# A hybrid mixer layer: one buffer for xdt and for B's two parts, and buffers of their own for B's returning tile and the transposed blocks

## The chip, the cores and the metric

The kernel runs on one core of a Trainium2 chip. The metric is the device time of one execution in microseconds, as the median of three runs. A profile is one further execution, taken by the hardware profiler.

## What is computed

One layer of a streaming encoder for two groups of requests that share the weights: 256 new positions of one stream and 16 positions of each of 8 running streams, 384 rows in all, with 2048 channels.

```python
u = rmsnorm(x);  proj = u @ w_in          # pool | z | xBC | dt | gates
a_pool = pooling of windows 2, 4, 8, 16, a map per group, a scale per channel
xbc = silu(causal_conv(xBC) + b)          # 4 taps; x: 4096 channels, B and C: 8 groups of 128
# for each chunk, group g, head r (8 groups, 8 heads of 64 channels each):
xdt = x * dt
y = einsum(cb * decay, xdt) + einsum(C, h) * exp(cum)
h = h * exp(last) + einsum(B, w_end, xdt)
y = y + d_skip * x
a_ssd = rmsnorm over each group of 512 (y * silu(z)) * ssd_norm
m = sig(gA) * (a_pool @ w_pool_proj) + sig(gB) * (a_ssd @ w_ssd_proj)
x = x + rmsnorm(m @ w_out);  x = x + rmsnorm(relu(rmsnorm(x) @ w_up)**2 @ w_down)
```

Outputs are the new x of both groups of requests and the new states of pooling, convolution and scan.

## The kernel before

All products are in float32, made of three matmuls of two parts each: every weight tile of 128x1024 is fetched by SP's queue (`wfetch`, line 63), its high part is written by ScalarE (`wh`, line 70), its low part by VectorE (`wl`, line 71), and `mm3` (lines 98 to 100) multiplies high by high, high by low and low by high. The tiles w, wh and wl have three buffers each. One projection (`proj`) takes two such weights, 24 matmuls each.

The profile's stage from about 430 us to 1210 us is a loop over the 8 groups of the scan (line 860). A group projects six convolution tiles (x 0, x 1, B, C, x 2, x 3) and four z tiles. TensorE's order is written out by hand: a chain (`last`, `lump`, `behind`) puts each block of small matmuls behind the projection before it. Each group has two such blocks:

- the middle block, after the projection of x 2: `t_pp` of the previous group's pair 1, `t_cb` (B times C), `t_yT` and `t_Y` of that pair, `t_yi` of this group's pair 0, and the state products `su` (`state`, line 794);
- the end block, after z 3: `t_pp`, `t_yT`, `t_Y` of pair 0, `t_yi` of pair 1, `su` of pair 0.

`finish(prev)` (line 842) stands after z tile 1. It normalises the previous group: TensorE sums over the partitions (`bc_g`, lines 196 and 197), VectorE reads that sum (`ssum<-bc_g`, line 199), takes ten Newton instructions (lines 182 to 186) and scales the four tiles `zs` (line 847).

Blocks of x and of B have to be transposed so that positions lie on partitions. `turned` does it in steps that `tick` runs, one after each weight of a projection: VectorE transposes blocks of 32x32 (`xb`, line 612), POOL's queue writes them to DRAM in four DMAs (line 617), and POOL's queue reads the whole tile back (line 623) into `xT` for x, and for B into the low half of `Bhl`. From `xT`, `xside` (line 742) makes `xdt` and `xhl` on VectorE, and sends a part of `xhl` through DRAM to `xst` on SP's queue. `bside` (line 706) splits B into `Bhl`'s two parts (ScalarE line 708, VectorE line 709) and sends a part through DRAM to `bst` in the same way. `mside` (line 729) reads the PSUM bank of `t_cb` into `cbm`. `eside` makes the decay matrices `E`, `dside` scales the old state `hs`.

All tiles of this stage come from the pool `pd`, which gives two buffers to a tag unless another number is named: two for `xdt`, two for `Bhl`, and two for `cacc`, which the convolution's taps (lines 593 to 598) and the transposed blocks `xb` share.

What is not in TensorE's chain is ordered by the framework's scheduler when the program is built: it orders each engine's queue by its own estimate of when inputs and buffers are ready. `later()` keeps an instruction behind the last split weight. On the chip every engine then takes its queue in this order.

Of the kernel before, what the change touches and what calls it, by code (L numbers as in the profile page):

```python
# [6 lines left out]
F32 = mybir.dt.float32  # L7
F32R = mybir.dt.float32r
I32 = mybir.dt.int32
AF = mybir.ActivationFunctionType  # L10
ALU = mybir.AluOpType
# [3 lines left out]
P = 128  # L15
T = 384
# [17 lines left out]
def build(ctx, tc, io):  # L34
    nc = tc.nc
    v, s, te, gp, sy = nc.vector, nc.scalar, nc.tensor, nc.gpsimd, nc.sync
# [13 lines left out]
    def mmtile(name):  # L50
        return psm.tile([P, 512], F32, tag="mm", name=name)
# [163 lines left out]
    def in_units(i):  # L215
        return [win[i - 5, 0], win[i - 5, 1]]
# [145 lines left out]
    with tc.tile_pool(name="phc", bufs=1, reuse_waits="tile") as pc, tc.tile_pool(name="phc2", bufs=2, reuse_waits="tile") as pc2:  # L362
        pst = pc.tile([P, KD, NB, 15], F32, name="pst")
        gp.dma_start(pst, io["state_pool"])
        bufs = []
        for i in range(2):
            b = pc.tile([P, 640], F32, name=f"pbuf{i}")[:, :519]
# [190 lines left out]
    with tc.tile_pool(name="phd", bufs=2, reuse_waits="tile") as pd, tc.tile_pool(  # L558
        name="phd1", bufs=1, reuse_waits="tile"
# [4 lines left out]
        for i in range(3):  # L564
            b = pd1.tile([P, 24, 19], F32, name=f"cbuf{i}")
# [38 lines left out]
        def conv(ui, c, tag, nb):  # L604
            return taps(conv_in(ui, c), c, tag, nb)

        def turned(src, i, o):
            xb, scr = [], t_scr[i]

            def turn():  # L610
                xb.append(pd.tile([P, T], F32, tag="cacc", name=f"xb{i}"))
                v.transpose(xb[0], src)

            def spread():
                for q in range(4):
                    p32 = slice(q * 32, q * 32 + 32)
                    gp.dma_start(
                        scr[:, p32].rearrange("(j a) b -> a j b", a=32),
                        xb[0][p32].rearrange("p (j b) -> p j b", b=32),
                    )  # L620

            wait = [lambda: None] if i < 32 else []
            steps.append(wait + [turn, spread, lambda: gp.dma_start(o, scr.rearrange("(b t) n -> t b n", b=3))])

        def xturned(D, g, j):
            S = D.p[j // 2]
            if j % 2 == 0:
                S.xT = pd.tile([P, 2, 3, P], F32, tag="xT", name=f"xT{S.nm}", bufs=1)
            turned(D.xs[j], g * 4 + j, S.xT[:, j % 2])
# [74 lines left out]
            return i  # L704

        def bside(D):
            bh, bl = (D.Bhl[:, a].rearrange("p b n -> p (b n)") for a in range(2))
            s.activation(bh, bl.bitcast(F32), AF.Copy)
            v.tensor_tensor(bl, bl.bitcast(F32), bh.bitcast(F32), ALU.subtract)
            bscr = b_scr[D.g]  # L710
            sy.dma_start(bscr, D.Bhl[:, :, 2, :].bitcast(F32))
            D.bs = bst[D.g % 2]
            for p4 in range(4):
                for h2 in range(2):
                    sy.dma_start(
                        D.bs[h2 * 64 + p4 * 16 : h2 * 64 + p4 * 16 + 16].bitcast(F32),
                        bscr.rearrange("(q h r) l n -> h l r q n", q=4, h=2)[h2, p4 // 2],
                    )
# [21 lines left out]
            )  # L740

        def xside(S):
            S.xdt = pd.tile([P, 2, 3, P], F32, tag="xdt", name=f"xdt{S.nm}")
            for q in range(2):
                tv = S.xT[:, q].rearrange("p b (h q) -> p b h q", h=2)
                for o, i in ((S.xdt, 3), (S.xT, 6)):
                    v.tensor_tensor(
                        o[:, q].rearrange("p b (h q) -> p b h q", h=2),
                        tv,
                        tok[:, i : i + 3, S.h0 + q * 2 : S.h0 + q * 2 + 2].unsqueeze(3).to_broadcast([P, 3, 2, 64]),  # L750
                        ALU.mult,
                    )
            S.xhl = pd.tile([P, 2, 2, 3, P], F32R, tag="xhl", name=f"xhl{S.nm}", bufs=1)
            s.activation(S.xhl[:, 0], S.xT, AF.Copy)
            v.tensor_tensor(S.xhl[:, 1], S.xT, S.xhl[:, 0].bitcast(F32), ALU.subtract)
            xscr = x_scr[S.qd]
            for l in range(2):
                sy.dma_start(xscr[:, l], S.xhl[:, l, :, 2, :].bitcast(F32))
            S.xst = pd.tile([P, 4, 2 * P], F32R, tag="xst", name=f"xst{S.nm}", bufs=1)
            for p4 in range(4):  # L760
                for h2 in range(2):
                    sy.dma_start(
                        S.xst[h2 * 64 + p4 * 16 : h2 * 64 + p4 * 16 + 16].bitcast(F32),
                        xscr.rearrange("(q h r) l j n -> h l r q (j n)", q=4, h=2)[h2, p4 % 2],
                    )
# [20 lines left out]
        def dside(S):  # L786
            v.tensor_tensor(
                S.hs.rearrange("p b (h q) -> p b h q", h=4),
                S.hs.rearrange("p b (h q) -> p b h q", h=4),
                decb[:, S.h0 : S.h0 + 4, :].rearrange("p h b -> p b h").unsqueeze(3).to_broadcast([P, NB, 4, 64]),  # L790
                ALU.mult,
            )
# [75 lines left out]
        for g in range(G + 1):  # L868
            if g == G:
                xside(prev.p[1])  # L870
                eside(prev.p[1], 0)
                eside(prev.p[1], 1)
                dside(prev.p[1])
                gate_b(0, pd, "hs")
                py = mmtile("pp_last")
                lump(lambda: t_pp(prev.p[1], py))
                lump(lambda: t_yT(prev.p[1]))
                lump(lambda: t_Y(prev.p[1]))
                state(prev.p[1])
                final(prev.p[1])  # L880
                gate_b(1, pd, "hs")
                finish(prev)
                break
            u0 = 17 + g * 10
            D = Pair()
            D.g = g
            D.p = [pair(D, jp) for jp in range(2)]
            D.xs, D.zs = [], []
            D.Bhl = pd.tile([P, 2, 3, P], F32R, tag="Bhl", name=f"Bhl{g}")
            D.xs.append(conv(u0, g * 4, "xs", 6))  # L890
            if g:
                xside(prev.p[1])
            xturned(D, g, 0)
            pload(D.p[0])
            if g:
                eside(prev.p[1], 0)
            D.xs.append(conv(u0 + 1, g * 4 + 1, "xs", 6))
            xturned(D, g, 1)
            if g:
                eside(prev.p[1], 1)  # L900
            D.BT = conv(u0 + 2, 32 + g, "BT", 2)
            turned(D.BT, 32 + g, D.Bhl[:, 1].bitcast(F32))
            if g:
                dside(prev.p[1])
            cload(D.p[0])
            D.CT = conv(u0 + 3, 40 + g, "CT", 2)
            cside(D)
            b2 = conv_in(u0 + 4, g * 4 + 2)
            S = D.p[0]
            S.py = mmtile(f"py{S.nm}")  # L910
            if g:
                lump(lambda: t_pp(prev.p[1], S.py))
            lump(lambda: t_cb(D))
            bside(D)
            if g:
                lump(lambda: t_yT(prev.p[1]))
                lump(lambda: t_Y(prev.p[1]))
            lump(lambda: t_yi(S))
            mside(D)
            yside(S)  # L920
            if g:
                state(prev.p[1])
                final(prev.p[1])
            D.xs.append(taps(b2, g * 4 + 2, "xs", 6))
            xside(S)
            xturned(D, g, 2)
            D.xs.append(conv(u0 + 5, g * 4 + 3, "xs", 6))
            xturned(D, g, 3)
            eside(S, 0)

            def zproj(j):
                ps = proj(in_units(u0 + 6 + j), xg, f"z{g}_{j}")
                z = pd.tile([P, T], F32, tag="zs", name=f"zs{g}_{j}", bufs=7)
                with later():
                    v.tensor_tensor(halves(z), even_odd(ps), halves(rstd), ALU.mult)
                    s.activation(z, z, AF.Silu)
                D.zs.append(z)

            zproj(0)
            pload(D.p[1])  # L940
            eside(S, 1)
            zproj(1)
            if g:
                finish(prev)
            zproj(2)
            dside(S)
            cload(D.p[1])
            zproj(3)
            S1 = D.p[1]
            S1.py = mmtile(f"py{S1.nm}")  # L950
            lump(lambda: t_pp(S, S1.py))
            lump(lambda: t_yT(S))
            lump(lambda: t_Y(S))
            lump(lambda: t_yi(S1))
            yside(S1)
            state(S)
            final(S)
            prev = D
# [92 lines left out]
    with tc.tile_pool(name="phf", bufs=1, side="right", reuse_waits="tile") as pf, tc.tile_pool(  # L1051
        name="phf2", bufs=2, side="right", reuse_waits="tile"
# [240 lines left out]
    with tc.tile_pool(name="phg", bufs=1, reuse_waits="tile") as pg, tc.tile_pool(  # L1293
        name="phg2", bufs=2, reuse_waits="tile"
# [8 lines left out]
        for c8 in range(NC):  # L1303
            hh = []
            for f8 in range(8):
                f = c8 * 8 + f8
# [172 lines left out]
```

## Time and profile before

| | |
|---|---|
| runs | 2692.59 us median of 3 (2689.98 to 2694.77) |
| profiled execution | 2697.46 us; span from its first to its last instruction 2695.3 us |
| mean granted clock of TensorE | 0.992 of full speed |
| TensorE busy | 2650.0 us, 98% of the span |
| VectorE, ScalarE, GpSimd busy | 1523.1, 1186.8, 269.6 us |

A line of the order of time gives the start in us from the span's start, how long the instruction (or the run of equal ones) lasted, the engine, the line of the kernel, the operation with output and inputs, and in brackets how long the engine had been idle before it and what ended that. A line of the waits gives the engine, what it was about to do, whom it waited for, the total in us, how often, and the longest. A line of a group gives count, busy time, mean ns, and the idle time before. A line of DMA issues ends with KB and the median us to landing.

### The profile page before, as it was taken

Reading aid. Unit: us, or ns where it says so; the run is one execution under the profiler, and the core shown is the slowest. Engines: PE = TensorE matmul, PEld = TensorE weight load, DVE = VectorE, ACT = ScalarE, POOL = GpSimd, SP = SyncE. Lnnn points to the kernel's source line nnn. Section 1 sums busy time; section 2 is a strip of 40 time slices with the busy share of each in tenths; the row PEclk is TensorE's granted clock in tenths of the full one; section 3 lists DMA queues with packets and bytes.
Section 4 is the critical chain, followed back from the end, with each engine's and each line's share of the span. In section 5 each row is a group of like instructions: output and inputs, shape, how many; then the busy total and the mean of one; then the engine's idle time right before and its main releaser. Section 6 shows DMA issues by size and latency. Waiting matters only on the chain.

```text
span 2695.3 us, 38595 instructions
## 1 busy us (share of the span) xinstructions
PE 2650.0 (98%) x15149; PEld 2468.2 (92%) x15149; DVE 1523.1 (57%) x2148; ACT 1186.8 (44%) x1834; POOL 269.6 (10%) x366
## 2 busy tenths in 40 slices
PE   9999999999999999999999999999999999999998
PEld 8998889999989999988888888989999999999897
DVE  6585336687887888866433345634444444444446
ACT  6443235466566665644322234633233333333233
POOL 0000001233233233321000000000000000000000
PEclk9999999999999999999999999999999999999999
DMA  7444446676766676666644455344444444444443
GB/s 270 152 133 158 145 150 212 202 224 214 237 216 227 222 249 211 224 211 227 217 156 157 156 187 155 126 135 139 133 136 138 133 136 138 133 134 139 134 134 132
DMA packets 153846, 467.10 MB, mean 173 GB/s; under 512 B 21121, under 2 KB 48321, under 8 KB 148673
## 3 DMA queue, kind: packets, MB, share of 16 engines
q1 hardware_dynamic: 134400, 389.90, 44.6%
q0 software_dynamic: 19264, 74.74, 7.9%
q8 instruction: 119, 1.95, 0.3%
q14 instruction: 63, 0.51, 0.1%
HBM read 414.97 MB, written 49.58 MB: 172 GB/s over the span
## 4 chain that ended last, share of the span: by engine, by line
PE 56%; DMA 1%; DVE 1%; POOL 0%; issue 0%; ACT 0%; DVEq 0%; POOLq 0%; ACTq 0%
PE pj_up L98 6%; PE pj_up L100 6%; PE pj_up L99 6%; PE wd L150 6%; PE wd L151 6%; PE wd L149 6%; PE pj_sp L151 3%; PE pj_sp L150 3%; PE pj_sp L149 3%; PE pj_gb L149 2%; PE wo L149 2%; PE wo L151 2%; PE pj_gb L150 2%; PE pj_gb L151 2%; PE wo L150 2%; DMA t_scr<-xb 1%
## 5 line engine op out<-in xcount | busy, mean ns | idle before, releaser
L98 PE MATMUL pj_up<-x1h,wh_up 128*128 128x384 f32 (+1 forms) x1024 | 334.1, 326 | 0.0
L99 PE MATMUL pj_up<-x1l,wh_up 128*128 128x384 f32 (+1 forms) x1024 | 333.9, 326 | 0.0
L100 PE MATMUL pj_up<-x1h,wl_up 128*128 128x384 f32 (+1 forms) x1024 | 333.8, 326 | 0.0
L71 DVE TENSOR_TENSOR wl_wd<-w_wd,wh_wd 128x1024 fp32r<-128x1024 f32 x126 | 154.4, 1225 | 240.3 <-ACT wh_wd L70 240.3
L151 PE MATMUL wd<-wh_wd,hl 128*128 128x512 f32 x756 | 286.8, 379 | 0.0
L150 PE MATMUL wd<-wl_wd,hh 128*128 128x512 f32 x756 | 286.8, 379 | 0.0
L149 PE MATMUL wd<-wh_wd,hh 128*128 128x512 f32 x756 | 286.8, 379 | 0.0
L70 ACT ACTIVATE wh_wd<-w_wd 128x1024 fp32r<-128x1024 f32 x126 | 133.1, 1056 | 322.2 <-PE wd L151 261.7
L70 ACT ACTIVATE wh_up<-w_up 128x1024 fp32r<-128x1024 f32 x126 | 133.1, 1057 | 291.8 <-PE pj_up L99 231.8
L98 PE MATMUL pj_x<-xgh,wh_x 128*128 128x384 f32 x768 | 256.2, 334 | 0.0
L71 DVE TENSOR_TENSOR wl_up<-w_up,wh_up 128x1024 fp32r<-128x1024 f32 x126 | 154.4, 1225 | 177.8 <-ACT wh_up L70 177.7
L100 PE MATMUL pj_x<-xgh,wl_x 128*128 128x384 f32 x768 | 254.0, 331 | 0.1
L99 PE MATMUL pj_x<-xgl,wh_x 128*128 128x384 f32 x768 | 254.0, 331 | 0.0
L99 PEld LDWEIGHTS pj_up<-x1l,wh_up 128*128 128x128 f32 x1024 | 194.0, 189 | 0.2
L98 PEld LDWEIGHTS pj_up<-x1h,wh_up 128*128 128x128 f32 x1024 | 194.0, 189 | 0.2
L100 PEld LDWEIGHTS pj_up<-x1h,wl_up 128*128 128x128 f32 x1024 | 194.0, 189 | 0.0
L100 PE MATMUL pj_z<-xgh,wl_z 128*128 128x384 f32 x512 | 170.9, 334 | 16.1 <-DVE wl_z L71 16.1
L98 PE MATMUL pj_z<-xgh,wh_z 128*128 128x384 f32 x512 | 169.7, 331 | 0.0
L99 PE MATMUL pj_z<-xgl,wh_z 128*128 128x384 f32 x512 | 169.6, 331 | 0.0
L71 DVE TENSOR_TENSOR wl_sp<-w_sp,wh_sp 128x1024 fp32r<-128x1024 f32 x64 | 78.4, 1225 | 154.0 <-ACT wh_sp L70 154.0
L151 PEld LDWEIGHTS wd<-wh_wd,hl 128*128 128x128 f32 x756 | 143.2, 189 | 20.0
L150 PEld LDWEIGHTS wd<-wl_wd,hh 128*128 128x128 f32 x756 | 143.2, 189 | 19.8
(335 smaller groups left out, 6044.9 us busy)
## 6 DMA issues: line engine op xcount, KB each, us to landing
w_up<-w_up SPq DMA_DIRECT2D x128, 512.0 KB, 3.3
w_wd<-w_down SPq DMA_DIRECT2D x128, 512.0 KB, 3.3
w_x<-w_in SPq DMA_DIRECT2D x96, 512.0 KB, 4.2
w_z<-w_in SPq DMA_DIRECT2D x64, 512.0 KB, 4.4
w_sp<-w_ssd SPq DMA_DIRECT2D x64, 512.0 KB, 3.3
w_ga<-w_ga SPq DMA_DIRECT2D x32, 512.0 KB, 3.4
w_pp<-w_pp SPq DMA_DIRECT2D x32, 512.0 KB, 3.3
hs<-ssm POOLq DMA_DIRECT2D x16, 1024.0 KB, 6.8
```

Source lines behind the costliest of these rows:

```text
L70: cut[0] = s.activation(h, w, AF.Copy)
L71: cut[1] = v.tensor_tensor(l, w, h.bitcast(F32), ALU.subtract)
L98: te.matmul(out, wh, xh, start=first, stop=False, **how)
L99: te.matmul(out, wh, xl, start=False, stop=False, **how)
L100: return te.matmul(out, wl, xh, start=False, stop=last, **how)
L149: te.matmul(out, mh, vh, start=k == 0, stop=False)
L150: te.matmul(out, mh, vl, start=False, stop=False)
L151: last[0] = te.matmul(out, ml, vh, start=False, stop=k == nk - 1)
```

## The change

The tag of the transposed blocks becomes `xb`, so that they have two buffers of their own and `cacc` serves the taps alone. `xdt` and `Bhl` have one buffer each. B's returning tile is no longer read into the low half of `Bhl`, but into a tile `Bt` of its own; `Bhl` is allocated only in `bside`, which writes both parts from `Bt`. The call of `bside` moves from the middle block, behind `t_cb`, to behind the convolution of x 3. Matmuls, DMAs and instructions are the same in number and size.

```diff
             def turn():
-                xb.append(pd.tile([P, T], F32, tag="cacc", name=f"xb{i}"))
+                xb.append(pd.tile([P, T], F32, tag="xb", name=f"xb{i}"))
                 v.transpose(xb[0], src)
...
         def bside(D):
-            bh, bl = (D.Bhl[:, a].rearrange("p b n -> p (b n)") for a in range(2))
-            s.activation(bh, bl.bitcast(F32), AF.Copy)
-            v.tensor_tensor(bl, bl.bitcast(F32), bh.bitcast(F32), ALU.subtract)
+            D.Bhl = pd.tile([P, 2, 3, P], F32R, tag="Bhl", name=f"Bhl{D.g}", bufs=1)
+            s.activation(D.Bhl[:, 0], D.Bt, AF.Copy)
+            v.tensor_tensor(D.Bhl[:, 1], D.Bt, D.Bhl[:, 0].bitcast(F32), ALU.subtract)
...
         def xside(S):
-            S.xdt = pd.tile([P, 2, 3, P], F32, tag="xdt", name=f"xdt{S.nm}")
+            S.xdt = pd.tile([P, 2, 3, P], F32, tag="xdt", name=f"xdt{S.nm}", bufs=1)
...
             D.xs, D.zs = [], []
-            D.Bhl = pd.tile([P, 2, 3, P], F32R, tag="Bhl", name=f"Bhl{g}")
             D.xs.append(conv(u0, g * 4, "xs", 6))
...
             D.BT = conv(u0 + 2, 32 + g, "BT", 2)
-            turned(D.BT, 32 + g, D.Bhl[:, 1].bitcast(F32))
+            D.Bt = pd.tile([P, 3, P], F32, tag="Bt", name=f"Bt{g}", bufs=1)
+            turned(D.BT, 32 + g, D.Bt)
...
             lump(lambda: t_cb(D))
-            bside(D)
...
             D.xs.append(conv(u0 + 5, g * 4 + 3, "xs", 6))
+            bside(D)
             xturned(D, g, 3)
```

## The prediction

> **What bounds the kernel now.** I read the page's engine row first, then who waited for whom on TensorE, then the order of time around each of those waits.
>
> ```profile
> PE 2650.0 (98%) x15149; PEld 2468.2 (92%) x15149; DVE 1523.1 (57%) x2148; ACT 1186.8 (44%) x1834; POOL 269.6 (10%) x366
> ...
> PE pj_z L100 <- DVE wl_z L71: 16.1, 7, 5.1
> PE su L802 <- DVE cbm L731: 14.9, 6, 4.7
> PE cb L652 <- ACT xs L601: 2.7, 2, 2.5
> ```
>
> TensorE sets the time. It waits in the group loop only, for three things: a low half of a z weight (7 waits, 16.1 us), the PSUM bank that `mside` reads (6 waits, 14.9 us) and a convolved tile (2.7 us). A change to buffers can save these waits and what hangs on them, and no more; it can also make new ones.
>
> How much hangs on them shows in the starts of the block's first product, `t_pp` (two blocks in a group, one after the x projections of four tiles, one at the group's end).
>
> ```profile
> 510.75 0.83 PE L696 MATMUL py<-xhl,Bhl 128*128 128x256 f32 x6
> 554.25 0.83 PE L696 MATMUL py<-xhl,Bhl 128*128 128x256 f32 x6
> ...
> 559.52 0.43 PE L98 MATMUL pj_x<-xgh,wh_x 128*128 128x384 f32 x1
> ...
> 583.19 0.33 PE L197 MATMUL bc_g<-nl_g,onesr 128*128 128x384 f32 x1
> 585.30 0.43 PE L100 MATMUL pj_z<-xgh,wl_z 128*128 128x384 f32 x1 [1.46 <-DVE wl_z L71]
> ...
> 600.68 0.83 PE L696 MATMUL py<-xhl,Bhl 128*128 128x256 f32 x6
> ...
> 681.02 0.33 PE L197 MATMUL bc_g<-nl_g,onesr 128*128 128x384 f32 x1
> 681.64 0.43 PE L100 MATMUL pj_z<-xgh,wl_z 128*128 128x384 f32 x1
> ...
> 1075.15 0.83 PE L696 MATMUL py<-xhl,Bhl 128*128 128x256 f32 x6
> 1118.65 0.83 PE L696 MATMUL py<-xhl,Bhl 128*128 128x256 f32 x6
> 1172.05 0.83 PE L696 MATMUL py<-xhl,Bhl 128*128 128x256 f32 x6
> ```
>
> From the end block to the middle block it is 43.50 us early and late in the loop (510.75 to 554.25, 1075.15 to 1118.65): nothing is lost there. From the middle block to the end block it is 46.43 us in group 1, of which the z wait takes 2.11 where an undisturbed group takes 0.62 (681.02 to 681.64); so 44.9 is the clean length. Groups 1 to 7 together take 1172.05 - 510.75 - 7 x 43.50 = 356.8 us for this stretch, against 7 x 44.9 = 314.6 clean. **42.2 us** are lost in these seven groups, more than the waits themselves.
>
> **Where the old waits come from.**
>
> ```profile
> 747.17 0.56 DVE L709 TENSOR_TENSOR Bhl<-Bhl 128x384 fp32r<-128x384 f32 x1 [4.44 <-ACT Bhl L708]
> ...
> 749.31 0.69 DVE L731 TENSOR_TENSOR cbm<-cb,cst 128x512 f32<-128x512 f32 x1
> ...
> 750.05 0.80 PE L802 MATMUL su<-xst,bst 64*128 64x256 f32 x3 [4.30 <-DVE cbm L731]
> ...
> 775.91 0.56 DVE L747 TENSOR_TENSOR xdt<-xT,tok 128x384 f32<-128x384 f32 x1 [4.07 <-DMA xT<-t_scr]
> 776.98 2.35 DVE L71 TENSOR_TENSOR wl_z<-w_z,wh_z 128x1024 fp32r<-128x1024 f32 x2
> ...
> 483.60 0.56 DVE L747 TENSOR_TENSOR xdt<-xT,tok 128x384 f32<-128x384 f32 x1 [4.54 <-DMA xT<-t_scr]
> ...
> 485.94 0.69 PE L100 MATMUL pj_z<-xgh,wl_z 128*128 128x384 f32 x1 [5.09 <-DVE wl_z L71]
> ...
> 489.30 0.33 PE L98 MATMUL pj_z<-xgh,wh_z 128*128 128x384 f32 x1
> ```
>
> VectorE takes its queue in order. At 747 it stands 4.44 us at `bside`'s split, whose input is still on its way through DRAM, and `cbm`, queued behind, comes out late; `su` needs the bank that `cbm` reads. At 776 and 484 it stands 4.07 and 4.54 us at `xside`'s product, whose transposed tile has not landed, with the low halves of the z weights behind it.
>
> **What the change removes.** On VectorE's queue in the changed program, `Bhl`'s split no longer stands ahead of `cbm`; it comes after the third tap of tile 2. The single `xdt` buffer keeps pair 1's product from being placed before the end block's `t_Y` has read pair 0's, so it stands behind the second read of Y in that block, when its tile has long landed. The `xb` tag lets a transposition go ahead without a free `cacc`. So VectorE stands at none of the three places any more. I take the whole 42.2 us of groups 1 to 7 away, and in group 0 the z wait of 5.09 us with its aftermath: 485.94 to 489.30 is 3.36 us for ten matmuls, which start 0.16 to 0.17 us apart elsewhere (1242.40 and 1242.57 below), 1.7 us too long, so 6.8 us. The wait for the convolved tile in group 0 stays: the order ahead of it is as before. Removed: 42.2 + 6.8 = **49.0 us**.
>
> **What the change adds.** The same scheduling that keeps `xdt` and `Bhl` back has moved something else. In the program before, VectorE's queue holds, after `nl_g` and pair 1's first product, the low halves of z tile 2's two weights, then zs 1, then the read of the norm's broadcast sum (`ssum<-bc_g`), with the Newton steps spread among later weights. In the changed program, in all seven groups with a `finish`, the queue reads: E, zs 0, `nl_g`, a transposition, `ssum<-bc_g`, the ten Newton instructions in one piece, two of the four scalings `zs<-zs,vec,ny_g`, and only then z tile 2's first low half. TensorE's queue is unchanged there: `bc_g` runs after z tile 1's last matmul and z tile 2's first follows it at once. TensorE therefore reaches its third z matmul 0.62 us after `bc_g`, and the weight for it is split behind a chain that starts from `bc_g`. Nothing can hide that chain; it is a new wait in each of seven groups, with a fixed length, whichever engine was early.
>
> Its length, from the same chain at the loop's end:
>
> ```profile
> 1242.40 0.33 PE L196 MATMUL bc_g<-nh_g,onesr 128*128 128x384 f32 x1
> 1242.57 0.33 PE L197 MATMUL bc_g<-nl_g,onesr 128*128 128x384 f32 x1
> ...
> 1242.93 0.56 DVE L199 TENSOR_SCALAR ssum<-bc_g 128x384 f32<-128x384 f32 x1 [1.89 <-PE bc_g L197]
> 1243.52 0.36 DVE L182 TENSOR_SCALAR ny_g<-ssum 128x384 int32<-128x384 int32 x1
> 1243.92 0.56 DVE L184 TENSOR_TENSOR na_g<-ny_g 128x384 f32<-128x384 f32 x1
> ...
> 1249.50 0.55 DVE L184 TENSOR_TENSOR na_g<-ny_g 128x384 f32<-128x384 f32 x1
> 1250.09 0.56 DVE L185 TENSOR_TENSOR na_g<-na_g,ssum 128x384 f32<-128x384 f32 x1
> ...
> 1251.28 2.21 DVE L847 SCALAR_TENSOR_TENSOR zs<-zs,vec,ny_g 128x384 f32<-128x384 f32 x4
> ...
> 1040.55 1.22 DVE L71 TENSOR_TENSOR wl_z<-w_z,wh_z 128x1024 fp32r<-128x1024 f32 x1
> ```
>
> `bc_g` to `ssum` 0.36; `ssum` to the first Newton instruction 0.59; that one to the next 0.40; nine dependent steps at 0.59 (1249.50, 1250.09, 1251.28) 5.31; two scalings at (2.21 - 0.61) / 3 = 0.53 each, 1.06; the split 1.22; TensorE's start behind it some 0.05. Sum 8.99 us, where 0.62 is the normal distance: **8.4 us** lost per group.
>
> A wait of that size has an aftermath. The rows at 485.94 and 489.30 gave 1.7 us; the 4.75 us wait of group 2 is followed by this:
>
> ```profile
> 654.88 0.69 PE L98 MATMUL pj_x<-xgh,wh_x 128*128 128x384 f32 x1
> ...
> 660.06 0.33 PE L99 MATMUL pj_x<-xgl,wh_x 128*128 128x384 f32 x1
> ```
>
> Sixteen matmuls in 5.18 us instead of 2.6: 2.6 us lost. I take the middle, 2.1 us. So each group pays 8.4 + 2.1 = 10.5, seven groups **73.5 us**. [...]
>
> **What is moved and costs nothing.** VectorE between `cbm` and z tile 0's second low half:
>
> ```profile
> 1029.45 0.69 DVE L731 TENSOR_TENSOR cbm<-cb,cst 128x512 f32<-128x512 f32 x1
> ...
> L787 DVE TENSOR_TENSOR hs<-hs,decb 128x2048 f32<-128x2048 f32 x16 | 36.6, 2289 | 0.0
> ...
> 758.82 6.12 SPq L762 DMA_DIRECT2D xst<-x_scr  x6
> w_z<-w_in SPq DMA_DIRECT2D x64, 512.0 KB, 4.4
> ```
>
> From 1029.45 to the end of the split at 1040.55 + 1.22 it is 12.3 us. The new queue takes the 2.29 us state scaling out of it and puts five 0.56 us instructions (two `xdt`, two `xT`, `Bhl`) and a transposition in: about 12.9. `cbm` can start about 2.3 us after the middle block's first product (its input 1.7 us, one split ahead), so the half is ready at 15.2; TensorE wants it at 5.27 (554.25 to 559.52) plus three halves of 24 matmuls at 0.16, 17.3. Two us to spare; if that cover were gone, each us over would cost one per group. On SP's queue, z tile 2's loads now stand behind `b_scr`, `x_scr`, eight `xst` and eight `bst` transfers. These can start once `xhl` is split, about 14 us after that product; with 4.4 us for a landing, 16 issues at up to 1.02 (6.12 / 6) and another 4.4 for the weight, it is there at 39 at the worst. The chain reaches its split at 28.9 + 7.7 = 36.7, so the cover holds unless the issues go at their slowest; at half of 1.02 the weight is there at 31. POOL's queue only takes the state load and some spreads in another order. The end block's VectorE gains three 0.56 us products and loses a 0.95 us split ahead of the next weight; the 43.50 us stretch has no wait today and I keep it.
>
> **The sum.** 73.5 - 49.0 = +24.5 us. The profiled execution took 2697.46 us (span 2695.3), 4.9 above the median of the runs, 2692.59; its waits for DMA may have been longer than theirs. Added to the profiled one it is 2722, to the median 2717. Since the new wait is fixed while the old ones vary, I take the place between: **2719 us**.
>
> **Rivals.** First, faster: the waits for DMA go and the Newton chain is covered, as would be if z tile 2's split stood ready before `bc_g`; then the whole 49 us are gained, 2644. It decides from the point where that split precedes `ssum` on VectorE's queue. Against it stands the queue's order in all seven groups; only if TensorE had other work between `bc_g` and z tile 2, 8 us of it, could the price vanish, and its queue has none. 0.05, and 0.03 that partial relief just balances it. Second, slower still: part of the old waits remains, with VectorE late at z tile 0 or `Bt` not landed when ScalarE's copy comes up, some 2 us a group with 0 to 1 of aftermath: 7 x 2 to 3 = 14 to 21, 2733 to 2740. For it speaks the cover of only 2 us; against it that the new wait lets VectorE's and SP's backlog drain in every group. 0.12. Third, SP: z tile 2's weight lands after the chain, by the 2 us at the worst above and a split: 7 x 3 = 21, 2740. 0.04. My forecast keeps 0.76.
>
> **Range and chances.** The low end is the median's sum with the short aftermath, 2717 - 3, less 8 for a chain that runs tighter and for the spread of the runs (2689.98 to 2694.77): 2706. The high end takes in the long aftermath and part of the second rival: 2738. A measurement of this kernel can tell about 0.2%, 5 us. Slower takes the forecast and the last two rivals, 0.92.
>
> **What would show it.** In the profile after: TensorE's waits for `cbm` gone; VectorE's waits for `xT` gone in groups 1 to 7; TensorE waiting seven times about 8 us at line 100 of `pj_z` for `wl_z`, some 58 us in all, each followed by matmuls of 0.53 us; the stretch from middle to end block near 55.4 us, the other still 43.5. I am wrong if that wait is below 5 us, or if waits at other lines add up to over 10 us.

## The result, and the profile after

The changed kernel takes **2719.35 us** (median of 4 runs, 2718.74 to 2722.5) against 2692.88 before (4 runs, 2689.98 to 2694.77): a ratio of 1.0102, 95% interval 1.0084 to 1.0119. The forecast was 2719. The profiled execution took 2718.74 us with a span of 2717.0, 21.7 more than the span before, where the forecast had 24.5.

The page's engine row and TensorE's waits in the group loop, changed kernel:

```profile
PE 2650.7 (98%) x15149; PEld 2466.1 (91%) x15149; DVE 1525.3 (56%) x2148; ACT 1166.5 (43%) x1820; POOL 272.3 (10%) x366
...
PE pj_z L100 <- DVE wl_z L71: 27.9, 8, 4.6
PE pj_z L98 <- ACT wh_z L70: 27.7, 8, 4.7
```

TensorE's busy time and its instructions are those of before (2650.0 us). The waits of `su` for `cbm` and of `cb` are gone. In their place stands a double wait in z tile 2: at line 98 for the high half of its first weight, at line 100 for the low half. The forecast had a single one, at line 100.

The order of time on TensorE, first products of the blocks, and `t_pp` of the loop's end:

```profile
501.68 0.83 PE L696 MATMUL py<-xhl,Bhl 128*128 128x256 f32 x6
545.18 0.83 PE L696 MATMUL py<-xhl,Bhl 128*128 128x256 f32 x6
600.24 0.83 PE L696 MATMUL py<-xhl,Bhl 128*128 128x256 f32 x6
...
1138.15 0.83 PE L696 MATMUL py<-xhl,Bhl 128*128 128x256 f32 x6
1193.59 0.83 PE L696 MATMUL py<-xhl,Bhl 128*128 128x256 f32 x6
1229.37 0.83 PE L696 MATMUL pp_last<-xhl,Bhl 128*128 128x256 f32 x6
```

From end block to middle block it is 43.50 us as before. From middle to end block it is 55.06 us in group 1 and 55.44 in group 7; the five between lie at 55.18 to 55.50. Together the seven take 1193.59 - 501.68 - 7 x 43.50 = 387.4 us, 30.6 more than before. Group 0 starts the count 510.75 - 501.68 = 9.07 us earlier, and the stretch behind the loop is 0.1 longer. 30.6 - 9.07 + 0.1 = 21.6, the whole difference of the spans.

One of these groups in the order of time, several engines:

```profile
742.42 0.83 PE L696 MATMUL py<-xhl,Bhl 128*128 128x256 f32 x6
...
760.50 5.12 SPq L762 DMA_DIRECT2D xst<-x_scr  x8
766.14 3.59 SPq L715 DMA_DIRECT2D bst<-b_scr  x7
769.84 1.36 SPq L63 DMA_DIRECT2D w_z<-w_in  x3
...
771.36 0.33 PE L197 MATMUL bc_g<-nl_g,onesr 128*128 128x384 f32 x1
771.73 0.56 DVE L199 TENSOR_SCALAR ssum<-bc_g 128x384 f32<-128x384 f32 x1 [4.61 <-PE bc_g L197]
...
773.72 1.06 ACT L70 ACTIVATE wh_z<-w_z 128x1024 fp32r<-128x1024 f32 x1 [7.00 <-DMA w_z<-w_in]
774.83 0.69 PE L98 MATMUL pj_z<-xgh,wh_z 128*128 128x384 f32 x1 [3.14 <-ACT wh_z L70]
...
778.05 1.15 DVE L847 SCALAR_TENSOR_TENSOR zs<-zs,vec,ny_g 128x384 f32<-128x384 f32 x2
779.12 1.22 DVE L71 TENSOR_TENSOR wl_z<-w_z,wh_z 128x1024 fp32r<-128x1024 f32 x1
780.39 0.69 PE L100 MATMUL pj_z<-xgh,wl_z 128*128 128x384 f32 x1 [4.55 <-DVE wl_z L71]
```

Read it from below. The matmul at 780.39 waits for the split at 779.12, which stands behind two scalings and the Newton chain, started by `bc_g` at 771.36: 9.03 us from `bc_g` to the matmul (9.02 to 9.21 in the seven groups). But the matmul at 774.83 had waited too. The z weight's fetch was issued at 769.84, 27.4 us after the middle block's first product, behind fifteen small reads that SP issued from 760.50 on; ScalarE, which waits for its landing, could start its copy at 773.72, 31.3 us after that product. TensorE had wanted the copy right behind `bc_g`, at 29.3. So two things are late in the same place, and the longer one, the chain, sets the price.

### The profile page after: what moved, and what is told of

Its sections match the earlier page's. It is cut to its first block, busy times and chain, and to the rows that moved or that the text cites. A ratio compares the mean times of both kernels' runs of the same rounds, so it can differ in the third digit from the quotient of the medians.

```text
span 2717.0 us, 38595 instructions
## 1 busy us (share of the span) xinstructions
PE 2650.7 (98%) x15149; PEld 2466.1 (91%) x15149; DVE 1525.3 (56%) x2148; ACT 1166.5 (43%) x1820; POOL 272.3 (10%) x366
## 4 chain that ended last, share of the span: by engine, by line
PE 94%; DVE 3%; ACT 1%; DMA 1%; issue 0%; POOL 0%; DVEq 0%; SPq 0%; ACTq 0%; POOLq 0%
PE pj_up L100 6%; PE pj_up L99 6%; PE pj_up L98 6%; PE wd L151 6%; PE wd L150 6%; PE wd L149 6%; PE pj_x L98 4%; PE pj_x L99 4%; PE pj_x L100 4%; PE pj_z L100 3%; PE pj_z L98 3%; PE pj_z L99 3%; PE pj_sp L150 3%; PE pj_sp L149 3%; PE pj_sp L151 3%; PE pj_gb L149 2%
## 5 line engine op out<-in xcount | busy, mean ns | idle before, releaser
L98 PE MATMUL pj_z<-xgh,wh_z 128*128 128x384 f32 x512 | 174.7, 341 | 27.7 <-ACT wh_z L70 27.7
L100 PE MATMUL pj_z<-xgh,wl_z 128*128 128x384 f32 x512 | 174.0, 340 | 27.9 <-DVE wl_z L71 27.9
L149 PEld LDWEIGHTS wd<-wh_wd,hh 128*128 128x128 f32 x756 | 142.9, 189 | 20.1
```

Of the source, the lines that this page charges most:

```text
L98: te.matmul(out, wh, xh, start=first, stop=False, **how)
L100: return te.matmul(out, wl, xh, start=False, stop=last, **how)
L149: te.matmul(out, mh, vh, start=k == 0, stop=False)
```

## Experiments

Two theories: the Newton chain ahead of the split is the cause (N), or the weight that the moved reads make late on SP's queue is (S), hidden under the chain in the changed kernel. All times stand against runs of the kernel before on the same chip: 2695.27 us median of 19 runs for the first four, 2694.72 of 7 for the others. The changed kernel's 2719.35 stands against 2692.88, so a difference between it and one of these runs is uncertain by some 2 us.

**The chain kept behind the splits** (changed kernel, and):

```diff
-        v.tensor_scalar(halves(hm), even_odd(o), -0.5 / n, -0.5 * EPS, ALU.mult, ALU.add)
+        with later():
+            v.tensor_scalar(halves(hm), even_odd(o), -0.5 / n, -0.5 * EPS, ALU.mult, ALU.add)
```

> The changed kernel, with the read of the norm's sum (ssum<-bc_g) held behind the last weight split that was asked for, so that VectorE's queue has z tile 2's two low halves ahead of the Newton chain; SP's queue is as in the changed kernel, with xst's eight and bst's seven reads ahead of z tile 2's loads. Theory N (the chain ahead of the split sets the wait): if it alone did, the whole 8.4 us and the slow matmuls behind it go, 7 x 10.5 = 73 us, to about 2646. Theory S (the weight itself lands late): its high half is ready some 3.9 us after TensorE asks, the low half 1.3 us after that, so 4 to 5 us of waiting and 1.5 to 2 us of slow matmuls stay in each group, 7 x 4 = 28 us gained, about 2691. I expect S's number, with the wait in one piece at line 98 and a short one at line 100.

Measured: 2693.71 us (10 runs), ratio 0.9993 (0.9983 to 1.0002). Its waits on TensorE and one group in the order of time (lines are one further down):

```profile
PE pj_z L98 <- ACT wh_z L70: 24.3, 7, 4.5
PE pj_z L100 <- DVE wl_z L71: 2.2, 7, 0.7
```

```profile
729.25 0.83 PE L697 MATMUL py<-xhl,Bhl 128*128 128x256 f32 x6
...
757.60 1.32 SPq L63 DMA_DIRECT2D w_z<-w_in  x3
...
761.70 2.26 ACT L70 ACTIVATE wh_z<-w_z 128x1024 fp32r<-128x1024 f32 x2 [8.14 <-DMA w_z<-w_in]
762.81 0.69 PE L98 MATMUL pj_z<-xgh,wh_z 128*128 128x384 f32 x1 [4.29 <-ACT wh_z L70]
```

The wait at line 100 shrinks to 2.2 us in all, and the time falls by some 26 us only. The weight, issued 28.4 us after the product, keeps TensorE waiting at line 98 by itself, 3.3 to 4.5 us in six groups; in group 1, where it leaves at 25.0, the wait is 0.6. In the group shown the stretch to the end block is 52.02 us where 44.9 was taken as clean: 4.5 us of waits, some 2.6 of aftermath.

**One Newton step in place of three in the group norm** (changed kernel; two of the three steps are left out, so the norm is less exact):

```diff
-    def newton(y, a, hm):
+    def newton(y, a, hm, n=3):
-        for _ in range(3):
+        for _ in range(n):
-        return newton(y, a, hm)
+        return newton(y, a, hm, 1)
```

> The changed kernel with one Newton step in place of three in the group norm (two thirds of the refinement are left out, so the norm is coarser). VectorE's queue then holds ssum, the first guess, three steps and four scalings ahead of z tile 2's split: 0.36 + 0.59 + 0.40 + 3 x 0.59 + 4 x 0.53 + 1.22 + 0.05 = 6.5 us from bc_g in place of 9.0. Theory N: 2.5 us a group less, 7 x 2.5 = 17.5, about 2702, line 100 reached 6.5 us after bc_g. Theory S (SP sets it): no change, 2719.

Measured: 2700.84 us (10 runs), ratio 1.0018 (1.0009 to 1.0028). The time falls by 18.5 us where the theory of the chain had 17.5, so the chain's length did set the price in the changed kernel. TensorE's waits show what the shorter chain uncovered:

```profile
PE pj_z L98 <- ACT wh_z L70: 31.0, 7, 5.1
PE pj_z L100 <- DVE wl_z L71: 6.5, 8, 1.6
```

Line 100 falls from 27.9 to 6.5 us, line 98 rises from 27.7 to 31.0: six steps off the chain bring it down onto the late weight.

**The reads behind z tile 2** (changed kernel; `xside` and `bside` keep what they write to DRAM, the reads back become functions of their own):

```diff
+        def bback(D):
+            bscr = b_scr[D.g]
             D.bs = bst[D.g % 2]
...
+        def xback(S):
+            xscr = x_scr[S.qd]
             S.xst = pd.tile([P, 4, 2 * P], F32R, tag="xst", name=f"xst{S.nm}", bufs=1)
...
             zproj(2)
+            xback(S)
+            bback(D)
             dside(S)
```

For pair 1 `xback` follows `xside` at once, as before.

> The changed kernel with the reads of xst (pair 0) and bst put behind z tile 2's projection in the program, nothing else. SP's queue then has z tile 2's first load behind one xst read instead of fifteen reads, and the scheduler by itself puts z tile 2's two low halves ahead of the Newton chain again. If the moved reads are the root of both waits, both go and nothing is left in the loop: 44.9 us from middle to end block, 2719.4 - 7 x 10.5 = about 2646, below both kernels. If the old waits (xT, Bhl) return, or the reads now come late for the end block's su, each would show as a wait at its line: 2655 to 2690.

Measured: **2647.37 us** (4 runs, 2645.47 to 2651.51), ratio 0.9821 (0.9807 to 0.9836): faster than both kernels. TensorE's waits, and one group (its middle block's first product is at 721.80):

```profile
PE pj_z L100 <- DVE wl_z L71: 2.1, 4, 1.5
```

```profile
741.22 0.38 SPq L63 DMA_DIRECT2D w_z<-w_in  x1
...
749.23 1.22 DVE L71 TENSOR_TENSOR wl_z<-w_z,wh_z 128x1024 fp32r<-128x1024 f32 x1 [0.59 <-ACT wh_z L70]
750.89 1.23 DVE L71 TENSOR_TENSOR wl_z<-w_z,wh_z 128x1024 fp32r<-128x1024 f32 x1 [0.44 <-ACT wh_z L70]
...
752.50 0.55 DVE L199 TENSOR_SCALAR ssum<-bc_g 128x384 f32<-128x384 f32 x1
```

The fetch leaves 19.4 us after the product, not 27.4. And the scheduler, with no order given to it on VectorE, puts both low halves of z tile 2 ahead of `ssum` again, in all seven groups. Moving sixteen reads in the program removed the late weight and the chain together. From middle block to end block it is now 44.70 us in five groups, 45.65 in group 3 and 47.62 in group 7.

**The transposed blocks back in `cacc`'s tag** (changed kernel, `tag="xb"` to `tag="cacc"`):

> The changed kernel with the transposed blocks back in the tag cacc; the order of every queue but for one place in SP's stays as in the changed kernel. Theory: the tag plays no part in the time, 2719 within 4 us. Rival: the tag is what lets the transpositions go early; without it each waits for a cacc and a spread's DMA, B's tile lands later, ScalarE stands longer at its copy, and the time goes up by 1 to 2 us a group, 2726 to 2735.

Measured: 2729.49 us (4 runs), ratio 1.0124 (1.0108 to 1.0139), some 10 us above the changed kernel. I had expected no difference. The rival of the expectation had this number, but from a loss in every group, and the loss is not spread: groups 1 to 7 have stretches of 55.3 to 55.6 us, within 0.3 of those in the changed kernel, but the first `t_pp` starts at 512.21, 10.5 us later. In group 0, in the order of time:

```profile
470.40 0.56 DVE L709 TENSOR_TENSOR Bhl<-Bt,Bhl 128x384 fp32r<-128x384 f32 x1 [5.19 <-ACT Bhl L708]
...
471.64 0.66 PE L98 MATMUL pj_x<-xgh,wh_x 128*128 128x384 f32 x1 [5.23 <-DVE cbuf L581]
```

B's transposition starts at 458.02 where the changed kernel has it at 452.89. `Bhl`'s split then stands 5.19 us on VectorE ahead of the read that empties a PSUM bank, and TensorE waits for the bank. In the changed kernel the same split stands 2.23 us in group 0, and no wait of TensorE follows there. A shared tag costs one late start at the head of the loop, then, and not something in each group.

**xdt's single buffer alone** (kernel before, and `bufs=1` for `xdt`):

> The kernel before with the single buffer for xdt alone; B's part and the transposed blocks stay as before. VectorE's queue then has ssum<-bc_g directly ahead of z tile 2's first low half, with the Newton steps spread behind it, and Bhl's split still ahead of cbm. On SP's queue bst's eight reads come early, as in the kernel before, so only xst's stand between xhl and z tile 2's weight. If it takes bst's reads behind xst to make that weight late: the wait at line 98 of pj_z stays under 1 us a group; line 100 waits 0.36 + 0.56 + 1.22 + 0.05 - 0.62 = 1.6 us a group; the wait of su for cbm stays near 15 us in all, the waits of VectorE for xT go; 2692.9 - 25 (z waits with aftermath, group 0) + 7 x 2 = 2680. If xst's reads alone make the weight late: line 98 waits some 4 us a group and the time is 2695 to 2705.

Measured: 2673.99 us (4 runs), ratio 0.9917 (0.9902 to 0.9932). Waits and one group:

```profile
PE su L802 <- DVE cbm L731: 10.4, 5, 3.0
PE pj_z L100 <- DVE wl_z L71: 10.1, 8, 1.5
```

```profile
733.73 0.83 PE L696 MATMUL py<-xhl,Bhl 128*128 128x256 f32 x6
...
738.15 3.68 SPq L715 DMA_DIRECT2D bst<-b_scr  x8
...
750.82 3.99 SPq L762 DMA_DIRECT2D xst<-x_scr  x8
754.91 3.35 SPq L63 DMA_DIRECT2D w_z<-w_in  x3
```

`bst`'s reads are issued by 742, `xst`'s come late, and the weight leaves 21.2 us after the product: line 98 waits 0.1 us at most in the seven groups. Where `su` still waits for `cbm` the weight leaves later, at up to 27.7 us, but TensorE comes later to it as well. At line 100 the wait is 1.1 to 1.5 us, for `ssum` alone is ahead of the split. The first expectation held, some 6 us too dear.

**B's part alone** (kernel before, with `Bt`, the single `Bhl` and `bside` moved as in the change):

> The kernel before with B's part alone (Bt, one Bhl, bside moved); two xdt, and xb in cacc's tag. VectorE's queue keeps z tile 2's first low half ahead of ssum, behind pair 1's product of the returned tile; Bhl's split is no longer ahead of cbm; on SP's queue bst's reads come behind xst's and ahead of z tile 2's weight. If the order on SP makes that weight late by itself: the wait of su for cbm (14.9 us) is gone, line 98 of pj_z waits 3 to 4 us a group, and the two nearly balance, 2685 to 2695. If the late weight needs the single xdt as well: only the wait for cbm goes, 2692.9 - 21 = 2672.

Measured: 2671.36 us (4 runs), ratio 0.9913 (0.9897 to 0.993). The first expectation, that the order on SP makes the weight late by itself, fell; the second held. Waits and one group (product at 726.06):

```profile
PE cb L652 <- ACT xs L601: 8.2, 7, 1.4
PE pj_z L100 <- DVE wl_z L71: 4.0, 9, 0.9
```

```profile
736.96 2.53 SPq L762 DMA_DIRECT2D xst<-x_scr  x3
...
745.56 5.89 SPq L715 DMA_DIRECT2D bst<-b_scr  x8
...
751.55 1.33 SPq L63 DMA_DIRECT2D w_z<-w_in  x3
```

Here `bst` is the late one and `xst` starts at 10.9; in the changed kernel `xst` starts at 18.1 and `bst`'s seven at 23.7. The weight leaves at 25.5, and no chain stands ahead of its split.

**Only `bst`'s reads moved** (changed kernel with `bback` but not `xback`):

> The changed kernel with only bst's reads moved in the program behind z tile 2; xst's stay. Seven of the eight bst reads leave the stretch ahead of z tile 2's weight on SP's queue; on VectorE ssum, two Newton steps and then z tile 2's first low half. If bst's reads make the weight late: it lands 3.6 us sooner, line 98 waits under 1 us, line 100 waits 0.36 + 0.56 + 0.40 + 0.59 + 1.22 + 0.05 - 0.62 = 2.6 us a group with about 1 of aftermath, so 2719.4 - 7 x (10.5 - 3.6) = 2671. If xst's eight reads are as bad: line 98 waits 3 us or more a group and the time is 2685 to 2700.

Measured: 2671.59 us (4 runs), ratio 0.9913 (0.9898 to 0.9928), as the theory of the reads had it. In one group (product at 728.19):

```profile
753.01 1.45 SPq L63 DMA_DIRECT2D w_z<-w_in  x3
...
756.78 1.06 ACT L70 ACTIVATE wh_z<-w_z 128x1024 fp32r<-128x1024 f32 x1 [4.30 <-DMA w_z<-w_in]
757.89 0.43 PE L98 MATMUL pj_z<-xgh,wh_z 128*128 128x384 f32 x1 [0.44 <-ACT wh_z L70]
760.23 0.43 PE L100 MATMUL pj_z<-xgh,wl_z 128*128 128x384 f32 x1 [1.74 <-DVE wl_z L71]
```

The weight leaves at 24.8, ScalarE's copy starts at 28.6, and TensorE waits 0.44. The start of the copy plus its 1.06 us less 29.3 gives the wait in this kernel (0.4), with the chain kept behind (4.2 against 4.29) and in the changed kernel (3.1 against 3.14). This group is one of the lightest: line 98 waits 0.3 to 2.5 us, under 1 us as expected in three groups of seven, 7.5 us in all.

**The reads moved in the kernel before**, with none of the change:

> The kernel before, with none of the change, but with xst's reads of pair 0 and bst's reads moved in the program behind z tile 2, as in the run of 2647 us. VectorE's queue then has z tile 2's first low half ahead of nl_g and of pair 1's product of the returned tile, whose wait now stands ahead of the second low half only; Bhl's split is still ahead of cbm. If moved reads help only where the change made a weight late: same as before, 2693. If they also loosen the kernel before, by letting that low half go ahead of the wait for xT: the z waits (16.1 us) and their aftermath go, the wait for cbm (14.9 us) stays, 2692.9 - 22 = 2671. If the buffers are not needed at all: 2647.

Measured: 2717.01 us (4 runs), ratio 1.0079 (1.0063 to 1.0095). All three expectations missed. Two lines of its waits:

```profile
PE su L808 <- DVE cbm L734: 13.9, 6, 5.5
DVE xdt L750 <- DMA xT<-t_scr: 77.1, 22, 7.5
```

VectorE's wait for `xT`, 53.9 us in the kernel before, grew to 77.1, and `nl_g`, queued behind it in group 7, made TensorE wait 6.3 us at `bc_g`. The blocks' writes to DRAM landed in 4.0 us median where it was 3.4. Weights that leave earlier then travel beside the transposed tiles; that this is what slows them was not tried apart. What follows is that the moved reads are worth nothing without the change's buffers.

## Why the prediction came out

**What bounds the kernel** was right: TensorE, losing only at a few places of the group loop.

**What the change removes** was a little undersized. Forecast: 49.0 us. The kernel with the reads moved has the change without its new wait, and gains 2695.27 - 2647.37 = 47.9 us, with some losses of its own left; the two parts alone gain 20.7 and 23.4. Its undisturbed stretch is 44.70 us, where 44.9 was taken as clean, so groups 1 to 7 had lost 356.8 - 7 x 44.70 = 43.9 us and not 42.2. Group 0 gave 9.07 us in place of 6.8. The wait of 2.46 us for the convolved tile was to stay there, since the order ahead of it is as before: the term was put at nothing, and the wait went. That makes 53.0 us. Which part takes the wait away is open: in group 0 it is 0.41 us with `xdt`'s single buffer alone and 1.00 with B's part alone, whose other 7.2 us of this wait stand in later groups.

**What the change adds** was right in size. The chain from `bc_g` to line 100 was worked out at 8.99 us and took 9.02 to 9.21; the stretch at 55.4 and took 55.06 to 55.50. That makes 30.6 us for groups 1 to 7 net, where 73.5 - 42.2 = 31.3 was forecast. Against the undisturbed stretch the new wait costs 387.4 - 7 x 44.70 = 74.5 us, forecast 73.5. The aftermath is 55.3 - 44.7 less the 8.6 lost before line 100 (9.1 us from `bc_g`, where an undisturbed group has 0.49), 2.0 a group; 2.1 was taken. VectorE's cover held: z tile 0's second low half is ready 15.5 to 16.7 us after the product, and TensorE uses it at 17.4.

**The sum**, 74.5 - 53.0 = 21.5 us by the spans against a forecast of 24.5, is right in kind. That the time came out within 1 us of 2719 is partly luck: the forecast was put between two sums, 2717 and 2722, and the medians differ by 26.5 us, the spans by 21.7.

**The step that failed is "the cover holds"** for the weight on SP's queue. Its landing was bracketed at 31 to 39 us after the block's first product, and ScalarE's copy starts at 31.3 to 32.8 in the seven groups. But it was compared with the time at which the chain reaches the split, 36.7. The first user of a weight is not the low half. It is ScalarE's copy for line 98, and TensorE wants that at 29.3. By the prediction's own test it was wrong there: the waits at line 100 were 4.6 us at most, and another line had 27.7 in all. The sum held because both waits lie in the same 9 us and TensorE did only two matmuls between them, so that together they make 7.7 to 8.3 us a group, close to the predicted 8.4. Had the chain not been there, the late weight would have cost nearly as much as the change removes: that is the run of 2693.71 us.

**The rivals.** The faster one, 2644 us with the split ahead of `ssum`, described the kernel at 2647.37 to within 4 us; it needed an order that the changed kernel doesn't have. The second did not come: no old wait is left in groups 1 to 7. The third, a late weight, was real but stood in the wrong place, under the chain and not behind it.

**What the prediction did not see** is that the loss belongs to neither part. Each part alone moves one set of reads back and leaves the other early, and each gains nearly 1%. Together `xdt`'s products and B's split come at the same time, both sets of reads stand in one piece ahead of the weight, and gains that add up to 44 us become a loss of 26. Why the scheduler puts thirteen instructions ahead of the split in that case stays partly open: it gave the chain up whenever the reads were gone (none ahead with all moved, three with `bst`'s moved), but B's part alone has the reads in front and no chain, and the scheduler's own estimates were not read.

## What to carry to other kernels

Compare the landing of a weight with its first user, the engine that reads it first, and not with the late consumer that you happen to be studying. Two lateness terms in one place hide each other: taking the longer away shows the next, so price each alone before calling the other covered. When buffers move producers, small reads that follow them on a queue move too; put those reads in the program behind the loads that are needed sooner, and the scheduler's order on other engines may come right by itself.

## What was not expected of the hardware

In two places of the traces the slow matmuls behind an idle time did not go by its length alone. Kernel before, then the kernel with `xdt`'s part alone, order of time on TensorE:

```profile
844.44 0.79 PE L802 MATMUL su<-xst,bst 64*128 64x256 f32 x3 [2.08 <-DVE cbm L731]
...
847.79 0.33 PE L100 MATMUL pj_x<-xgh,wl_x 128*128 128x384 f32 x1
```

```profile
830.90 0.49 PE L802 MATMUL su<-xst,bst 64*128 64x256 f32 x3 [2.02 <-DVE cbm L731]
```

An idle time of 2.08 us was followed by matmuls of 0.53 us until 847.79, 3.35 us long; one of 2.02 us by full speed at once. Here are both places in stretches of 3.41 us: bounds, length, TensorE's busy time and its matmuls, the granted clock, and share and rate of the DMA engines.

```profile
840.86:844.27 3.41, 1.50 (x25) 1.00 0.57 190
844.27:847.68 3.41, 3.24 (x11) 0.50 0.81 236
```

```profile
826.06:829.47 3.41, 2.83 (x65) 1.00 0.17 50
829.47:832.88 3.41, 1.98 (x12) 1.00 0.60 184
```

The idle time of 2.08 us fell almost wholly into one of these stretches, in which TensorE was idle for 56%, and the granted clock was 0.50 in the next. That of 2.02 us was divided between two, idle for 17% and 42%, and the clock was 1.00 in both.

In the traces of the two kernels, from 430 to 1240 us, the granted clock was 1.00 or 0.50, and half clock came sixteen times: for 3.41 us (seven times), 6.83 (three) and 10.24 (six). In the 3.41 us ahead of it TensorE had been idle for 56 to 100% in fifteen cases and was busy for 1.59 us of it in one (1124.16 to 1127.58 us, kernel before); 3.41 us with 1.61 busy, from 572.84 on in the changed kernel, were followed by full clock. The two idle times above differ in how they fell into the stretches shown and hardly in length; what makes the clock change is not shown by these traces.
